# The down product of a feed-forward layer as one level of Strassen's seven block products, and a reordered entry

## The chip, the core and the metric

The kernel runs on one core of a Trainium2 chip. The core has a matrix engine (TensorE, PE in the profile, with its weight loads as PEld), VectorE (DVE), ScalarE (ACT), GpSimd (POOL), and DMA queues that several engines issue; most loads here are issued by SyncE (SP). Each engine works through its own instructions in order, and semaphores tie the engines together. The metric is the device time of one execution in microseconds (us), lower is better: the median of several runs, beside one execution that was profiled.

## What is computed

One layer of a decoder, 512 tokens, model width 2048, all in float32. Everything up to `x + mixed @ w_out` is attention and is left alone by the change; the feed-forward behind it is what matters here (D_FF is 5632):

```python
x = x + mixed @ w_out[l]
h = rmsnorm(x, ln_ffn[l])
gate, up = jnp.split(h @ w_gate_up[l], 2, axis=-1)
x = x + (jax.nn.silu(gate) * up) @ w_down[l]
return rmsnorm(x, ln_final)
```

So "gate and up" is a product of 512 x 2048 by 2048 x 11264, and "down" one of 512 x 5632 by 5632 x 2048.

## The kernel before

**Precision by splitting.** TensorE multiplies in float32r, which keeps fewer bits than float32. Each operand is therefore split into `hi`, its value rounded to float32r, and `lo`, the rest; a product is three matmuls, hi x hi, lo x hi and hi x lo. ScalarE writes `hi` (a Copy), VectorE writes `lo` (a subtraction). A matmul takes a stationary operand of 128 x 128 (`lhsT`), which a weight load brings in, and a moving one of 128 rows and up to 512 columns (`rhs`), and adds into a PSUM bank of 128 x 512.

**Order.** The framework schedules instructions by itself, except those that were pinned to program order: `dma`, and everything issued through `pV`, `pA`, `pG`, `pT` (class `Pinned`, L106 to L118; pinned instructions all carry line L118 in the profile, pinned DMAs L100). The feed-forward is pinned nearly throughout. Exceptions that matter are `rstd_from` (L258) and `row_bc` (L273). Buffers come from pools; a tile of a pool with the option `reuse_waits="tile"` waits for those tiles alone that lay on the same memory before. A pool lays out its tags in the order of their first use.

**Entry of the feed-forward.** The output projection ends in `add_outB` (L933): the residual sum stands in four tiles `x2[c]` of 512 columns (pool `v8`) and is stored to scratch memory `x2s[c]`, the last one on ScalarE's queue (L942). `h2_split` (L887) transposes `x2` on TensorE and scales it to `xh`. `form(p, s)` (L908) makes from `xh` the left sides of the seven products, for half s of the inner dimension, hi and lo side by side in one tile of 512 columns; `form_tile` (L901) says where each lies: for s = 0 those of "1", "7", "2", "5" in `act8` tiles and "4", "6", "3" in three tiles `s8`. `rstd2_make` (L963) computes the norm's row factors on VectorE and ScalarE; `rstd2_bc` spreads them over the partitions with `row_bc`: four diagonal tiles `dg` (VectorE, two buffers), a matmul with `ones` for each, and a copy out (ScalarE). Memory of `v8` is then taken over by pool `ff` (tags `raw2`, `t`, `hct`).

**Gate and up.** This is already one level of a Strassen scheme (Winograd's variant), with products named "1" to "7", in 44 units of 128 gate columns and the 128 up columns that go with them (`Unit`, L984). A unit takes seven slots, one per product in the order `PR` = 1, 7, 2, 5, 4, 6, 3 (NS = 308 slots in all). In each slot `product` issues 8 matmuls of 512 and 8 of 256 columns. The weights of the four blocks ("11", "12", "21", "22") are loaded into `raw` (pool `wp`, 3 buffers) and `raw2`; four right sides are differences that GpSimd makes (`sum`: "7" = 22 − 12, "5" = 12 − 11, "6" = 22 − "5", "4" = 21 − "6"). For each product ScalarE writes the rounded weights twice, to SBUF (`to_hi`, the stationary operand) and to PSUM (`to_hp`, 2 buffers), and VectorE subtracts the latter from the source (`to_lo`). In slot n run hi and lo of n + 1, hp of n + 2 and the product of n. The results are taken out of the banks by the methods `get_...`, added up by `fold` (GpSimd), and go through `gate`, `silu`, `scale_up`, `act`; `store` writes them to scratch memory `aT`. The loop over n at the end of the section has this order written out by hand.

**Down.** `add_down` queues, for 11 groups of 512 inner rows and four chunks c of 512 columns, slabs of 256 rows. The groups come back from `aT` (`load_act`), and are split by `split_act`. `add_tok` (L324) issues for each token block t and each 128 inner rows three matmuls of 512 columns into one bank (L336 to L338); `done` adds the banks into `x2[c]`, which `load_x2` has brought back. `split` (L192) makes hi (L200) and lo (L201) of the weights. The eleventh group comes last, t by t (L1307 to L1309), each t followed by the final norm (`last_col`) and the stores of its rows.

Of the kernel before, what the change touches and what calls it, by code (L numbers as in the profile page):

```python
# [37 lines left out]
def tile_hymba(ctx: ExitStack, tc: tile.TileContext, x, ln_mix, w_in, sb_norm, swa_norm,  # L38
# [234 lines left out]
    def row_bc(col, name, pb=None):  # L273
        pb = pz() if pb is None else pb
        for t in range(NT):
            dg = sm.tile([P, P], F32, tag="dg", name="dg", bufs=2)
            V.tensor_scalar(out=dg, in0=ident, scalar1=col[:, t:t + 1], scalar2=None, op0=ALU.mult)
            mm(pb[:, t * P:(t + 1) * P], lhsT=ones, rhs=dg, start=(t == 0), stop=True,
               skip_group_check=True)
# [880 lines left out]
    def add_down(n):  # L1160
        for c in range(4):
            r0 = n * GF * P

            def done(t, pb, c=c):
                xc = x2[c][:, t, :]
                V.tensor_tensor(out=xc, in0=pb, in1=xc, op=ALU.add)
# [174 lines left out]
```

## Time and profile before

| | us |
|---|---|
| runs, median of 3 | 2109.63 |
| lowest, highest | 2109.22, 2110.27 |
| the profiled execution | 2110.75 |
| its span, first to last instruction | 2109.0 |

| busy in the profiled execution | us | share of the span |
|---|---|---|
| TensorE matmuls | 2072.3 | 98% |
| VectorE | 1489.1 | 71% |
| ScalarE | 1235.1 | 59% |
| GpSimd | 677.7 | 32% |

Counted on TensorE's timeline, the feed-forward begins at 733 us, the down product at 1612 us and its last group at 2056 us. In the rows of the profile, `out<-in` names the tiles written and read, `xN` counts instructions, and a bracket at the end of a timeline row gives the engine's idle time before it and what ended that. `z`, `m` and `o` are the PSUM banks. Rows of matmuls overlap by half, so a matmul's share of time is the distance of two starts, not the row's duration.

### The profile page before, as it was taken

Reading aid. Unit: us, or ns where it says so; the run is one execution under the profiler, and the core shown is the slowest. Engines: PE = TensorE matmul, PEld = TensorE weight load, DVE = VectorE, ACT = ScalarE, POOL = GpSimd, SP = SyncE. Lnnn points to the kernel's source line nnn. Section 1 sums busy time; section 2 is a strip of 40 time slices with the busy share of each in tenths; the row PEclk is TensorE's granted clock in tenths of the full one; section 3 lists DMA queues with packets and bytes.
Section 4 is the critical chain, followed back from the end, with each engine's and each line's share of the span. In section 5 each row is a group of like instructions: output and inputs, shape, how many; then the busy total and the mean of one; then the engine's idle time right before and its main releaser. Section 6 shows DMA issues by size and latency. Waiting matters only on the chain.

```text
span 2109.0 us, 28765 instructions
## 1 busy us (share of the span) xinstructions
PE 2072.3 (98%) x10634; PEld 1760.4 (83%) x10634; DVE 1489.1 (71%) x1953; ACT 1235.1 (59%) x1773; POOL 677.7 (32%) x415
## 2 busy tenths in 40 slices
PE   8999999999999989999999999999999999999998
PEld 7888888888788868888888888888887888888886
DVE  3358888769935778888788788788777545545565
ACT  5347777557723467777777777777775222222232
POOL 0014444200000146666666666666662000000000
PEclk9999999999999989999999999999999999999999
DMA  5332222222242435534544544553454433333332
GB/s 180 91 89 66 66 62 69 73 78 81 85 155 93 156 88 129 135 105 121 135 114 111 135 124 107 130 133 103 125 135 170 165 120 120 120 117 127 127 130 80
DMA packets 285516, 239.94 MB, mean 114 GB/s; under 512 B 10368, under 2 KB 236736, under 8 KB 282816
## 3 DMA queue, kind: packets, MB, share of 16 engines
q1 hardware_dynamic: 284960, 235.97, 37.9%
q8 instruction: 84, 1.38, 0.3%
q0 software_dynamic: 176, 1.06, 0.1%
q10 hardware_dynamic: 240, 1.07, 0.1%
q14 instruction: 56, 0.46, 0.1%
HBM read 218.14 MB, written 19.92 MB: 113 GB/s over the span
## 4 chain that ended last, share of the span: by engine, by line
PE 91%; DVE 4%; DMA 2%; issue 1%; ACT 1%; SPq 0%; POOLq 0%; DVEq 0%; ACTq 0%
PE o L118 22%; PE m L118 17%; PE m L368 4%; PE m L369 4%; PE m L370 4%; PE z L338 4%; PE z L337 4%; PE z L336 4%; PE m L337 4%; PE m L336 4%; PE m L338 4%; PE o L336 3%; PE o L337 3%; PE o L338 3%; DMA raw<-in_w_down_dram 1%
## 5 line engine op out<-in xcount | busy, mean ns | idle before, releaser
L200 ACT ACTIVATE whi<-raw 128x1024 fp32r<-128x1024 f32 x184 | 194.6, 1058 | 435.8 <-PE o L338 204.2
L201 DVE TENSOR_TENSOR wlo<-raw,whi 128x1024 fp32r<-128x1024 f32 x184 | 227.9, 1238 | 287.2 <-ACT whi L200 284.6
L118 POOL TENSOR_TENSOR t<-raw,t 128x1024 f32<-128x1024 f32 x88 | 224.1, 2547 | 270.0 <-ACT hp L118 180.9
L118 DVE TENSOR_TENSOR wlo<-t,hp 128x1024 fp32r<-128x1024 f32 x176 | 214.3, 1218 | 111.9 <-PE o L118 70.4
L118 ACT ACTIVATE whi<-t 128x1024 fp32r<-128x1024 f32 x176 | 186.6, 1060 | 95.1 <-PE o L118 59.8
L118 POOL TENSOR_TENSOR t<-raw,raw 128x1024 f32<-128x1024 f32 x86 | 208.8, 2429 | 52.2 <-DVE wlo L118 43.1
L118 DVE TENSOR_TENSOR wlo<-raw,hp 128x1024 fp32r<-128x1024 f32 x132 | 159.9, 1211 | 43.2 <-issue 38.9
L118 PE MATMUL m<-hca,whi 128*128 128x512 f32 x704 | 185.4, 395 | 4.7 <-ACT whi L118 4.5
L118 PE MATMUL o<-hca,whi 128*128 128x512 f32 x704 | 184.7, 394 | 0.0
L118 ACT ACTIVATE hp<-t 128x1024 fp32r<-128x1024 f32 x176 | 178.1, 1012 | 2.4 <-POOL t L118 2.4
L118 ACT ACTIVATE whi<-raw 128x1024 fp32r<-128x1024 f32 x132 | 139.3, 1055 | 58.4 <-PE m L118 55.0
L368 PE MATMUL m<-hhi,whi 128*128 128x512 f32 x416 | 169.1, 407 | 0.9 <-DVE swv L256 0.9
L369 PE MATMUL m<-hlo,whi 128*128 128x512 f32 x416 | 163.1, 392 | 0.0
L370 PE MATMUL m<-hhi,wlo 128*128 128x512 f32 x416 | 162.8, 391 | 0.0
L118 PEld LDWEIGHTS m<-hca,whi 128*128 128x128 f32 x704 | 127.6, 190 | 28.3 <-ACT whi L118 4.9
L118 PEld LDWEIGHTS o<-hca,whi 128*128 128x128 f32 x704 | 127.5, 190 | 22.8
L118 DVE TENSOR_TENSOR w<-w,rbc 128x512 f32<-128x512 f32 x88 | 139.4, 1585 | 2.3 <-POOL w L118 2.3
L118 ACT ACTIVATE hp<-raw 128x1024 fp32r<-128x1024 f32 x132 | 133.2, 1009 | 3.6 <-DMA raw<-in_w_gate_up_dram 3.0
L337 PE MATMUL z<-wlo,ah 128*128 128x512 f32 x320 | 124.6, 389 | 0.0
L338 PE MATMUL z<-whi,al 128*128 128x512 f32 x320 | 124.5, 389 | 0.0
L336 PE MATMUL z<-whi,ah 128*128 128x512 f32 x320 | 124.2, 389 | 0.0
L118 POOL TENSOR_TENSOR w<-c 128x1024 f32<-128x1024 f32 x44 | 106.8, 2427 | 14.3 <-ACT whi L200 14.3
(318 smaller groups left out, 4952.5 us busy)
## 6 DMA issues: line engine op xcount, KB each, us to landing
raw<-in_w_gate_up_dram SPq DMA_DIRECT2D x352, 256.0 KB, 5.2
raw<-in_w_down_dram SPq DMA_DIRECT2D x36, 1024.0 KB, 5.1
raw<-in_w_in_dram SPq DMA_DIRECT2D x40, 512.0 KB, 3.6
raw<-in_w_in_dram SPq DMA_DIRECT2D x64, 256.0 KB, 3.2
raw<-in_w_out_dram SPq DMA_DIRECT2D x32, 512.0 KB, 3.9
aT<-w SPq DMA_DIRECT2D x44, 256.0 KB, 3.5
araw<-aT SPq DMA_DIRECT2D x11, 1024.0 KB, 7.2
raw<-in_w_down_dram SPq DMA_DIRECT2D x16, 512.0 KB, 6.5
```

Of the source, the lines that this page charges most:

```text
L118: return lambda *a, **k: tc.keep_in_program_order(fn(*a, **k))
L200: ih = A.activation(out=hi, in_=raw, func=AF.Copy)
L201: il = V.tensor_tensor(out=lo, in0=raw, in1=f(hi), op=ALU.subtract)
L336: mm(o, lhsT=lh[:, sl], rhs=hi[:, j, :], start=first, stop=False, skip_group_check=halves)
L337: mm(o, lhsT=lh[:, sl], rhs=lo[:, j, :], start=False, stop=False, skip_group_check=halves)
L338: mm(o, lhsT=ll[:, sl], rhs=hi[:, j, :], start=False, stop=(k == nslab * a - 1), skip_group_check=halves)
L368: mm(o, lhsT=wh, rhs=xh, start=(k == 0), stop=False)
L369: mm(o, lhsT=wh, rhs=xl, start=False, stop=False)
L370: mm(o, lhsT=wl, rhs=xh, start=False, stop=(k == KT - 1))
```

## The change

**Down.** The first ten groups become five pairs of groups, and each pair two passes: pass d takes groups 2(d // 2) and 2(d // 2) + 1 as its two inner blocks, and two chunks of 512 columns, so 1024 columns, as its two column blocks; the tokens are split into halves of 256. Of each inner block of 512 rows the weights come in two chunks i of 256 rows. A pass is 14 slots: seven products in the order `PD` = 1, 7, 6, 4, 5, 2, 3, with two chunks each, and 12 matmuls of 512 columns in a slot. It uses the machinery of the units (`Weights` holds what both share): GpSimd makes four sums of each chunk, ScalarE and VectorE hi, hp and lo. `take` adds the banks into x2, or into `vv` for product "6"; `add_v` adds `vv` to the other three quarters at the end. `Left` makes the left sides: it loads two groups from `aT`, forms the differences in place, and splits them into `act8` tiles `dca`; for the first pair these operations stand on VectorE up to product "4", later mostly on GpSimd. The eleventh group stays as it was and has its weights and its left side loaded and split during pass 9.

**The order.** What to issue in which slot now comes from a table (`at_slot`, `run`), with the stages load, sum, product, take and late, for units and passes alike; slot NS is the first of pass 0. Within the units the slots of the single steps stay as they were, save that the last unit's steps come earlier and that its `fold` is on VectorE. Loads of pass 0 and of its left side start in slot NS − 6.

**The entry.** `form_tile` puts "5", "4", "6", "3" of s = 0 in `act8`, and "1", "7", "2" in `s8`. The first unit's block "21" goes to `raw` in place of `raw2`, and is issued behind sum "5". `rstd2_bc` comes behind product 8 in place of product 7, and its four `dg` are made by ScalarE.

The core of the diff:

```diff
     def row_bc(col, name, pb=None):
-        pb = pz() if pb is None else pb
+        act = pb is not None
+        pb = pb if act else pz()
...
+            if act:
+                A.activation(out=dg, in_=ident, func=AF.Copy, scale=col[:, t:t + 1])
...
     def form_tile(p, s):
         if s == 0:
-            return (act8("hca") if p in "1725" else
+            return (act8("hca") if p in "5463" else
...
-                   if q in ("11", "22") or self.j == 0 and q != "21" else ft("raw2", [P, 8, P], F32, 3))
+                   if q in ("11", "22") or self.j == 0 else ft("raw2", [P, 8, P], F32, 3))
...
-            pG.tensor_tensor(out=self.w4[:, 0:2, :].rearrange("p a (h b) -> p (a h) b", h=2), in0=self.c[:, :, 0:256],
+            (pG if self.j < NFF - 1 else pV).tensor_tensor(out=self.w4[:, 0:2, :].rearrange("p a (h b) -> p (a h) b", h=2), in0=self.c[:, :, 0:256],
...
+    PD = ("1", "7", "6", "4", "5", "2", "3")
+    class Pass(Weights):
...
+        def sum(self, p, i):
+            a, b = {"7": ("22", "12"), "5": ("12", "11"), "6": ("22", "T5"), "4": ("21", "T6")}[p]
...
+            pG.tensor_tensor(out=t, in0=self.raw[a, i], in1=self.t[b[1], i] if b[0] == "T" else self.raw[b, i],
+                             op=ALU.subtract)
...
+        def product(self, pi):
+            p, i = pi
+            if i == 0 and p in "1752":
+                get = (pm, po)[(self.d + (p in "72")) % 2]
+                self.bank[p] = [get(), get()]
+            on = {"6": "1", "4": "7", "3": "5"}.get(p)
+            bk = self.bank[on or p]
+            hi, lo = self.hi.pop(pi), self.lo.pop(pi)
+            x = dc[self.g, p]
+            for part, w in ((0, hi), (256, hi), (0, lo)):
+                for e in range(2):
+                    for t in range(2):
+                        c = part + t * P
+                        pT.matmul(bk[t], lhsT=x[:, 2 * i + e, c:c + P], rhs=w[:, e, :],
...
+        def take(self, p):
...
+            for t in range(2):
...
+                pV.tensor_tensor(out=out, in0=bk[t], in1=out, op=ALU.add)
...
+    class Left:
...
+        def diff(self, eng):
+            self.s3 = ft("t", [P, 4, 256], F32, 3)
+            eng.tensor_tensor(out=self.s3, in0=self.block("11"), in1=self.block("21"), op=ALU.subtract)
...
+        def hi(self, p):
+            dc[self.g, p] = act8("dca")
+            pA.activation(out=dc[self.g, p][:, :, 0:256], in_=self.src(p), func=AF.Copy)
+        def lo(self, p, eng):
+            hl = dc[self.g, p]
+            eng.tensor_tensor(out=hl[:, :, 256:512], in0=self.src(p), in1=f(hl)[:, :, 0:256], op=ALU.subtract)
...
+    for c in range(4):
+        at_slot(NS + (-4, -3, 3, 4)[c], "load", load_x2, c)
+    for d in range(10):
+        b0, u = NS + 14 * d, passes[d]
+        for q, k in (("11", -6), ("12", -5), ("22", -3), ("21", 0)):
+            at_slot(b0 + k, "load", u.load, q, 0)
+            at_slot(b0 + k + (q != "11"), "load", u.load, q, 1)
+        for k, p in ((-3, "5"), (-1, "7"), (1, "6"), (3, "4")):
+            at_slot(b0 + k, "sum", u.sum, p, 0)
+            at_slot(b0 + k + 1, "sum", u.sum, p, 1)
+        for k, p in enumerate(PD):
+            at_slot(b0 + 2 * k + 2, "take", u.take, p)
+    for g in range(5):
+        b0, l = NS + 28 * g, lefts[g]
+        for k in range(2):
+            at_slot(b0 + (-16 if g else -6) + k, "load", l.load, k)
+        if g:
+            order = ((-10, l.hi, "1"), (-9, l.lo, "1", pG), (-8, l.diff, pG), (-7, l.hi, "7"), (-7, l.s1, pG),
+                     (-6, l.lo, "7", pG), (-5, l.s2, pG), (-4, l.hi, "6"), (-3, l.lo, "6", pV), (-2, l.hi, "4"),
+                     (-1, l.lo, "4", pV))
+        else:
+            order = ((-3, l.hi, "1"), (-3, l.lo, "1", pV), (-2, l.diff, pV), (-1, l.hi, "7"), (-1, l.lo, "7", pV),
+                     (0, l.s1, pV), (1, l.s2, pV), (2, l.hi, "6"), (2, l.lo, "6", pV), (3, l.hi, "4"),
+                     (4, l.lo, "4", pV))
+        for k, fn, *args in order + ((4, l.hi, "5"), (5, l.lo, "5", pG), (5, l.hi, "2"), (6, l.lo, "2", pG),
+                                     (7, l.s4, pG), (8, l.hi, "3"), (9, l.lo, "3", pG)):
+            at_slot(b0 + k, "late", fn, *args)
...
+    at_slot(5, "late", rstd2_make)
+    at_slot(8, "late", rstd2_bc)
...
+    units[0].sum("5")
     units[0].load("21")
-    sums(1)
+    units[0].sum("6")
     form("2", 1)
     of(2, "to_hp")
-    for n in range(NS):
+    for n in range(NS + ND):
```

More of the change, by code (lines that the diff above doesn't have):

```diff
@@ L1174, in tile_hymba, with at_slot, run @@
-    down0 = len(queue)
-    for n in range(NG - 1):
-        if n == NG - 2:
-            last_from = len(queue)
-        add_down(n)
-    def load_x2(c):
-        x2[c] = xp.tile([P, NT, 512], F32, tag="x2", name="x2r", bufs=4)
-        dma(out=x2[c], in_=x2s[c])
+    plan = {}
+    def at_slot(n, stage, fn, *args):
+        plan.setdefault((n, stage), []).append((fn, args))
+    def run(n, stage):
+        for fn, args in plan.pop((n, stage), ()):
+            fn(*args)
+    for j in range(NFF):
+        b0, u = 7 * j, units[j]
+        for q in ("22", "12", "11"):
+            at_slot(b0 - 5, "load", u.load, q)
+        at_slot(b0 - 3, "load", u.load, "21")
+        for k, p in enumerate("7564"):
+            at_slot(b0 - 2 + k, "sum", u.sum, p)
+        late = j < NFF - 1
+        for k, fn in ((1, u.get_p1), (2, u.get_p7), (3 if j else 5, u.get_c11), (4, u.get_p75), (6, u.get_u2),
+                      (6, u.get_c22), (7, u.get_c12), (9 if late else 7, u.fold), (10 if late else 8, u.gate),
+                      (11 if late else 8, u.silu), (11 if late else 9, u.scale_up), (12 if late else 9, u.act),
+                      (13 if late else 9, u.store)):
+            at_slot(b0 + k, "take", fn)
@@ new lines, in load_x2 @@
+    def load_x2(c):
+        x2[c] = (side.tile([P, NT, 512], F32, tag="s8", name="x2r", bufs=3) if c < 2 else e8("x2r"))
+        dma(out=x2[c], in_=x2s[c])
+    for c in range(4):
[10 more added lines that the diff above has]
+            at_slot(b0 + 2 * k + 2, "take", u.take, p)
@@ L1184, in tile_hymba @@
+    at_slot(4, "late", form, "3", 1)
+    at_slot(5, "late", rstd2_make)
+    at_slot(8, "late", rstd2_bc)
+    at_slot(NS + 9, "late", lambda: tc.keep_in_program_order(A.preload_act_table_set("natural_log_exp_and_others")))
+    for k in [k for k in plan if k[0] < 0 or k == (0, "sum")]:
+        del plan[k]
+    units[0].sum("5")
     units[0].load("21")
-    for n in range(3, 5):
-        loads(n)
-    sums(1)
+    units[0].sum("6")
     form("2", 1)
     of(2, "to_hp")
-    for n in range(NS):
-        j, k = divmod(n, 7)
-        loads(n + 5)
-        sums(n + 2)
+    for n in range(NS + ND):
+        if n > 1:
+            run(n, "load")
@@ L1194, in tile_hymba @@
         if n:
+            run(n, "sum")
             of(n + 1, "to_hi")
@@ L1200, in tile_hymba @@
         of(n, "product")
[L1201 to L1242 removed]
+        run(n, "take")
+        run(n, "late")
+    run(NS + ND, "take")
+    run(NS + ND, "late")
     open_z("psz2")
[L1246 to L1249 removed]
     gf = const.tile([P, D], F32, tag="swv", name="gf")
```

250 lines of the change are left out of this document (132 added, 118 removed).

## The prediction

> **What bounds the kernel now.** I read the page first, then the busy time by stretches, then TensorE's timeline, and only then the waits at the two places where TensorE stops.
>
> ```profile
> span 2109.0 us, 28765 instructions
> PE 2072.3 (98%) x10634; PEld 1760.4 (83%) x10634; DVE 1489.1 (71%) x1953; ACT 1235.1 (59%) x1773; POOL 677.7 (32%) x415
> PE 91%; DVE 4%; DMA 2%; issue 1%; ACT 1%; SPq 0%; POOLq 0%; DVEq 0%; ACTq 0%
> ...
> 800.00:1600.00 800.00, 800.00 (x4584) 704.02 (x4583) 656.34 (x656) 628.95 (x697) 501.36 (x205) 1.00 0.46 121
> 1660.00:2050.00 390.00, 389.33 (x1717) 321.71 (x1716) 206.73 (x240) 98.21 (x95) 0.00 (x0) 1.00 0.37 124
> 736.00:777.00 41.00, 30.56 (x142) 25.02 (x141) 31.19 (x33) 24.12 (x30) 18.46 (x7) 0.83 0.43 116
> ```
>
> TensorE holds 91% of the chain that ended last. In the stretches (columns: length, then busy time of PE, PEld, DVE, ACT, POOL, granted clock, DMA share, GB/s) it is never idle from 800 to 1600 (gate and up) and hardly from 1660 to 2050 (down). In the first of these VectorE is busy for 82% of the time, ScalarE for 79%, GpSimd for 63%, and still TensorE does not wait; in the second VectorE has 53% and ScalarE 25%. So in the down stage a matmul taken away is time taken away, and three engines have room there. From 736 to 777, the entry of the feed-forward, TensorE idles for 10 us and its clock is 0.83.
>
> The price of a matmul is the distance of starts, since the rows' durations overlap. The first and the last of 101 starts in the down stage, and one slot of gate and up:
>
> ```profile
> 1990.20 0.39 PE L336 MATMUL z<-whi,ah 128*128 128x512 f32 x1
> ...
> 2012.87 0.39 PE L337 MATMUL z<-wlo,ah 128*128 128x512 f32 x1
> ...
> 1100.66 2.79 PE o L118 x16
> ```
>
> (2012.87 − 1990.20)/100 = 0.2267 us for 512 columns. A slot of gate and up has 8 matmuls of 512 and 8 of 256 columns in 2.793 us (308 slots).
>
> **The change, part by part.**
>
> *Matmuls.* Down has 11 groups of 4 x 4 x 4 x 3 = 192 matmuls of 512 columns, 2112 in all. The ten passes replace ten groups: 7 products x 2 chunks x 12 = 168 each, 1680 instead of 1920. The last group keeps its 192. So 240 go: 240 x 0.2267 = **−54.4 us**. The columns of one matmul stay at 512, and one stationary load stands before each, as now. A pass alternates between two banks at each matmul; in the stretch from 1660 to 2050 the bank changes at each third matmul and the distance stays 0.2267, so I take nothing for it.
>
> The Trainium skill, "TensorE: Matmul & The Clock Gate", section "Back-to-back issue gap", gives 131 ns for a sustained stream of 512 columns; by that figure the 240 would be worth an estimated 31.4 us. The trace's 226.7 ns is for these very matmuls and decides.
>
> *Can the other engines feed the passes?* A slot of a pass is 12 x 0.2267 = 2.72 us. Its work, by these rows:
>
> ```profile
> L118 ACT ACTIVATE hp<-t 128x1024 fp32r<-128x1024 f32 x176 | 178.1, 1012 | 2.4 <-POOL t L118 2.4
> L118 ACT ACTIVATE whi<-t 128x1024 fp32r<-128x1024 f32 x176 | 186.6, 1060 | 95.1 <-PE o L118 59.8 <-PE m L118 34.3 <-PE o L338 1.0
> L118 DVE TENSOR_TENSOR wlo<-t,hp 128x1024 fp32r<-128x1024 f32 x176 | 214.3, 1218 | 111.9 <-PE o L118 70.4 <-PE m L118 41.6
> L118 POOL TENSOR_TENSOR t<-raw,t 128x1024 f32<-128x1024 f32 x88 | 224.1, 2547 | 270.0 <-ACT hp L118 180.9 <-DVE wlo L118 78.1 <-DMA raw<-in_w_gate_up_dram 5.9
> L118 POOL TENSOR_TENSOR t<-raw,raw 128x1024 f32<-128x1024 f32 x86 | 208.8, 2429 | 52.2 <-DVE wlo L118 43.1 <-ACT hp L118 6.7 <-DMA raw<-in_w_gate_up_dram 2.4
> L1166 DVE TENSOR_TENSOR x2r<-z,x2r 128x512 f32<-128x512 f32 x80 | 53.0, 685 | 24.1 <-PE z L338 20.3 <-DMA x2r<-x2s 3.8
> L118 DVE TENSOR_TENSOR w<-w,rbc 128x512 f32<-128x512 f32 x88 | 139.4, 1585 | 2.3 <-POOL w L118 2.3
> ...
> 1603.79 0.68 DVE L118 TENSOR_TENSOR w<-w,rbc 128x512 f32<-128x512 f32 x1
> ```
>
> ScalarE: 1.01 + 1.06, and 7 copies for the left side in 28 slots, 7 x 1.06/28 = 0.27: 2.34 us, 86%. VectorE: 1.22, one add (0.69) on average, and two subtractions in 28 slots, some 0.15: 2.06, 76%. GpSimd: 16 sums and 9 left operations in 28 slots, 25 x 2.49/28 = 2.22, 82%. All lie under 2.72. Sums come one slot before their use, one in each of 13 slots in a row at most; the adds into x2 wait for a product that ended as their slot begins, and the bank is wanted two slots later, so the split queued behind them on VectorE is not held. Loads are 5.24 MB a pass, 138 GB/s, near the 121 of gate and up. I take **0** for the 140 slots; bounds 0 and one slot a pass (27 us), if jitter eats GpSimd's lead.
>
> *Entry of the feed-forward.* Today:
>
> ```profile
> 733.25 1.17 PE L118 MATMUL m<-hca,whi 128*128 128x512 f32 x4 [0.24 <-ACT junk L118]
> ...
> 742.19 3.78 PE L118 MATMUL m<-hca,whi 128*128 128x512 f32 x8 [3.12 <-ACT whi L118]
> ...
> 747.48 2.32 PE L118 MATMUL o<-hca,whi 128*128 128x512 f32 x8
> ...
> 760.90 1.19 PE L118 MATMUL m<-hca,whi 128*128 128x512 f32 x4 [1.36 <-ACT whi L118]
> ...
> 764.96 0.68 PE L278 MATMUL m<-dg,ones 128*128 128x128 f32 x4
> 769.24 0.80 PE L278 MATMUL m<-dg,ones 128*128 128x128 f32 x2 [3.59 <-DVE dg L277]
> 771.53 0.80 PE L278 MATMUL m<-dg,ones 128*128 128x128 f32 x2 [1.50 <-DVE dg L277]
> 771.98 2.05 PE L118 MATMUL o<-hca,whi 128*128 128x512 f32 x4
> ...
> 776.47 2.00 PE L118 MATMUL m<-hca,whi 128*128 128x512 f32 x8
> ...
> 731.35 3.89 DMA x2s<-x
> ...
> 735.74 3.36 DMA raw<-in_w_gate_up_dram
> ...
> 726.13 4.75 POOL L118 TENSOR_TENSOR t<-raw 128x1024 f32<-128x1024 f32 x2 [26.52 <-DMA raw<-in_w_gate_up_dram]
> ...
> 759.46 0.20 ACT L262 ACTIVATE rl<-rv 128x4 f32<-128x4 f32 x1 [3.49 <-DVE rv L260]
> ...
> 737.34 1.22 DVE L118 TENSOR_TENSOR xh<-xh 128x1024 f32<-128x1024 f32 x1
> ...
> 772.37 0.60 ACT L281 ACTIVATE rbc<-m 128x512 f32<-128x512 f32 x1 [7.48 <-PE m L278]
> ```
>
> Slot 9 begins at 776.47; nine slots after 733.25 it would be 758.39, so 18.1 us are lost: 3.3 before slot 2, some 2.8 in slots 2 and 3 at half speed (8 matmuls of 512 columns take 3.8 us), 3.2 around slot 7, 7.0 for the row broadcast (764.96 to 771.98), 1.7 in slot 8, again at half speed.
>
> Slot 2 waits for block "21". Its load began when the store of x2[3] ended (731.35 + 3.89 = 735.24), because raw2, the first tile that pool `ff` hands out, lies on the memory of x2[3]. The change puts "21" into `raw`, to be free when sum "5" has read "11". But now sum "5" takes the first tile of `ff`, and I expect the wait to move to GpSimd: sum "5" at 735.3 instead of 728.5, done at 737.8; load 0.5 + 3.4, to 741.5; hp, the form's copy and whi 0.95 to 1.06 each: slot 2 at 744.5, **+2.3**. Queued behind it on GpSimd is only sum "6", which reads "5" anyway; on SP nothing due before slot 2. If the tile lies elsewhere, form "5" is late next (its add ends at 738.6, copy and whi 2.1): 740.7, −1.5. Starting later, TensorE works less of the half-speed stretch (it ends near 748: the eight from 747.48 take 2.3 us, whole ones at full speed 2.0): −1.0. The 3.2 stay: that chain (rstd2 between VectorE and ScalarE) is not touched.
>
> The row broadcast's four `dg` go from VectorE, where they waited behind other work and GpSimd, to ScalarE, behind slot 8. ScalarE shows no 128-column copy here; between its 0.2 us for 4 and 0.6 for 512 columns I take 0.3. Two buffers: two matmul pairs 0.4, two `dg` 0.6, two pairs 0.4, the copy out 0.6 before product 9 gets its bank, with hand-overs some 2.2 instead of 7.0: −4.8, and slot 8 at full clock −1.7. Together **−5.2**, bounds +2 and −13.
>
> *Entry of down.* Today:
>
> ```profile
> 1620.24 11.03 DMA raw<-in_w_down_dram
> ...
> 1627.80 0.39 PE L338 MATMUL o<-whi,al 128*128 128x512 f32 x1
> 1632.48 1.22 PE L336 MATMUL m<-whi,ah 128*128 128x512 f32 x2 [4.30 <-ACT whi L200]
> ...
> 1639.28 0.40 PE L336 MATMUL o<-whi,ah 128*128 128x512 f32 x1
> ...
> 1612.92 3.25 POOL L118 TENSOR_TENSOR w<-c 128x1024 f32<-128x1024 f32 x1 [14.31 <-ACT whi L200]
> ...
> 1625.00:1630.00 5.00, 3.18 (x15) 2.29 (x13) 4.00 (x6) 2.00 (x2) 0.00 (x0) 1.00 1.00 412
> 1630.00:1635.00 5.00, 2.48 (x5) 1.57 (x6) 2.07 (x2) 1.06 (x1) 0.00 (x0) 0.72 1.03 419
> ```
>
> A weight block comes 11 us after its issue, with the 16 DMA engines full at 412 to 419 GB/s; TensorE stops for 4.7 us and then runs at half speed (clock 0.72 in the window behind). From 1627.80 to 1639.28 are 16 starts, 3.6 us by rights: 7.9 us lost. In the new order (NS is the first slot of pass 0) the loads start six slots ahead: 7.3 MB from slot NS−6 to NS−2. At 412 GB/s that is 17.8 us and 2 of latency, against 16.8 to slot NS; the last block, "22", wanted there by sum "7", comes some 2 us late, about what the lead allows.
>
> VectorE is worse off. Because GpSimd makes a sum in each slot from NS−3 to NS+4, the first left side goes to VectorE (7 operations), and so does the last fold. In these 8 slots (22 us) it has 8 splits (9.8), 8 operations from PSUM (5.5), 5 of gate, up and product (3.4 alone) and 8 of 1024 elements (9.8): 28.4. The 13 that read and write SBUF only also wait for GpSimd: w<-w,rbc takes 1.585 on average, and 0.68 when GpSimd is idle (1603.79), so 0.9 more each, 11.7. That is 6 to 18 us too much, less the 3.3 of lead that a split has (it is wanted two thirds into the next slot: 2.72 + 1.81 − 1.22). So 3 to 15 lost; I take 10, and 1 for a chance of half clock: 11 instead of 7.9, **+3.1**. ScalarE's copies of the left side wait for VectorE there, and the next slot's whi stands behind them: the same lag, counted once. The store behind VectorE on SP holds up only x2r loads due 12 slots later.
>
> *The rest.* The last group's weights are split during pass 9 (VectorE and ScalarE under 90%), and GpSimd's load of the last gain now stands behind `al`; VectorE may wait for it some us while TensorE has four free banks, 10.9 us. 0; if that cover were gone, some 3.
>
> Sum: −54.4 − 5.2 + 3.1 = −56.5. The profiled execution took 2110.75 us (span 2109.0), the median of the runs is 2109.63, 1.1 lower. 2110.75 − 56.5 = 2054.25, less 1.1: **2053.1 us**.
>
> **Rivals.** (1) *Both entries run clean*: entry −13, down −5: 2109.6 − 54.4 − 18 = 2037 us. For it: the DMAs start earlier than today. Against: VectorE's 28 us in 22. (2) *The passes lag a slot each* (GpSimd at 82% must keep a strict order, each operation behind the one that waits): +27, or half of that: 2067 to 2080. Against: in gate and up three engines at 82, 79 and 63% cost nothing. (3) *Slower: GpSimd becomes the bound of every pass.* It has 12.5 operations a pass; at 2.49 they take 31 of 38.1 us. From (38.1 + 5.6)/12.5 = 3.5 us each on, ten passes cost the 56 us saved and the change loses; at 3.6 it is 2122. The one of 3.25 (at 1612.92), beside VectorE's splits from SBUF, shows that such durations occur; the means of 2.43 and 2.55 speak against it. (4) *The bank changes slow the stream*: if TensorE paused between banks often enough to be put to half clock for a third of the passes, 381 us would grow by 127: 2180. The row from 800 to 1600 speaks against it: banks change each slot, clock 1.00. The Trainium skill tells of such a case in "TensorE: Matmul & The Clock Gate", section "A second HAM failure mode: psum-queue depth-cycling". (5) *It gives nothing*: the same loss in size as the gain, within 4 us of 2109.6.
>
> **Chances.** Forecast, 2046 to 2062: 0.60. Rival 1, 2035 to 2046: 0.13. Rival 2, 2062 to 2085: 0.19. Rival 3: 0.04. Rival 4: 0.02. Rival 5: 0.02. The range leaves out rivals 3 to 5 (0.08), the cleanest quarter of rival 1 (0.03) and the upper third of rival 2 (0.07): 2038 to 2076. Faster by over 0.2% (about what can be told from no change here): 0.92; within it 0.02; slower 0.06.
>
> **What would show it.** In the profile after: 1872 down matmuls at 0.2267 us; slots of 2.72 us with TensorE busy throughout ten passes; sum "5" of the first unit beginning only after x2s<-x landed; `dg` on ScalarE and a broadcast of some 2 us; VectorE without a gap from NS−3 to NS+6 and TensorE waiting for wlo there. Wrong if TensorE shows a stop in each pass (released by POOL or ACT), or if the distance of starts in a pass is over 0.23.

## The result and the profile after

The changed kernel takes **2062.53 us** (median of 4 runs, 2062.20 to 2062.63) where the kernel before took 2109.95 beside it (4 runs): a ratio of 0.9775, 95% interval 0.9758 to 0.9792. The prediction was 2053.1 with a range of 2038 to 2076: the sign and the range hold, the forecast is 9.4 us too low. The time lies 0.5 us outside the band of 2046 to 2062 that the prediction gave a chance of 0.60, in the band of its rival 2, whose lag in each pass does not show below. The profiled execution took 2062.63 us.

From the page of the changed kernel, then the stretches (length, then busy time of PE, PEld, DVE, ACT, POOL, granted clock, DMA share, GB/s):

```profile
PE 2018.5 (98%) x10394; PEld 1713.1 (83%) x10394; DVE 1484.6 (72%) x1986; ACT 1441.0 (70%) x1992; POOL 1007.0 (49%) x539
```

```profile
1608.00:1640.00 32.00, 23.20 (x83) 16.48 (x83) 31.86 (x25) 18.12 (x20) 22.64 (x9) 0.89 0.52 186
1660.00:1926.00 266.00, 266.00 (x1175) 220.31 (x1174) 194.55 (x204) 214.86 (x221) 216.98 (x88) 1.00 0.41 140
1926.00:1969.00 43.00, 40.30 (x169) 32.38 (x169) 34.83 (x32) 30.32 (x32) 30.39 (x13) 0.96 0.30 94
```

TensorE is 98% busy as before, so the share tells nothing; the stretches do. It is never idle from 1660 to 1926, where VectorE, ScalarE and GpSimd are busy for 73, 81 and 82%. It idles in the first pass, where VectorE has 31.86 of 32 us, and around 1960.

TensorE's timeline of the changed kernel (a bracket is the idle time before the row, and what ended it):

```profile
732.52 1.16 PE L118 MATMUL m<-hcs,whi 128*128 128x512 f32 x4 [0.24 <-ACT junk L118]
...
744.24 2.07 PE L118 MATMUL m<-hcs,whi 128*128 128x512 f32 x4 [5.91 <-ACT whi L118]
...
749.53 2.05 PE L118 MATMUL o<-hca,whi 128*128 128x512 f32 x8
...
767.22 1.16 PE L118 MATMUL o<-hcs,whi 128*128 128x512 f32 x4
...
770.18 0.78 PE L282 MATMUL m<-dg,ones 128*128 128x128 f32 x4
...
772.62 1.20 PE L118 MATMUL m<-hcs,whi 128*128 128x512 f32 x4 [0.69 <-ACT rbc L285]
...
1607.93 0.39 PE L118 MATMUL m<-whi,dca 128*128 128x512 f32 x1
...
1617.54 2.11 PE L118 MATMUL o<-whi,dca 128*128 128x512 f32 x8 [2.44 <-ACT whi L118]
...
1624.30 3.78 PE L118 MATMUL o<-whi,dca 128*128 128x512 f32 x8 [2.06 <-ACT whi L118]
...
1659.49 0.84 PE L118 MATMUL o<-whi,dca 128*128 128x512 f32 x3
...
1926.05 1.98 PE L118 MATMUL m<-whi,dca 128*128 128x512 f32 x8
...
1963.75 1.25 PE L118 MATMUL m<-wlo,dca 128*128 128x512 f32 x4 [2.44 <-DVE wlo L118]
1964.79 3.56 PE L118 MATMUL m<-whi,dca 128*128 128x512 f32 x8
1968.19 1.09 PE L118 MATMUL m<-wlo,dca 128*128 128x512 f32 x4
1969.11 1.98 PE L118 MATMUL o<-whi,dca 128*128 128x512 f32 x8
...
2008.04 0.39 PE L1428 MATMUL z<-lhi,ah 128*128 128x512 f32 x1
```

The rows that start a pass give its length. A pass of 168 matmuls at 0.2267 us takes 38.08 us; what is over is its **loss**. Pass 0 runs from 1607.93 to 1659.49, 51.56 us: loss 13.5. Passes 1 to 7 take 1926.05 − 1659.49 = 266.56 us = 7 x 38.08: no loss. Pass 8 takes 43.06, loss 5.0; pass 9 38.93, loss 0.85. Rows on the other engines of the changed kernel around the stops:

```profile
730.62 0.36 ACTq L946 DMA_DIRECT2D x2s<-x  x1
...
734.76 2.40 POOL L118 TENSOR_TENSOR t<-raw 128x1024 f32<-128x1024 f32 x1 [7.03 <-PE m L118]
...
1613.06 5.71 POOL L118 TENSOR_TENSOR t<-raw,raw 128x1024 f32<-128x1024 f32 x2 [1.57 <-DMA raw<-in_w_down_dram]
1618.73 6.12 POOL L118 TENSOR_TENSOR t<-raw,ty 128x1024 f32<-128x1024 f32 x2
...
1616.46 3.40 DVE L118 TENSOR_TENSOR xd<-xd 128x1024 f32<-128x1024 f32 x1
1619.78 1.21 DVE L118 TENSOR_TENSOR wlo<-t,hp 128x1024 fp32r<-128x1024 f32 x1
...
1622.56 3.38 DVE L118 TENSOR_TENSOR xd<-xd 128x1024 f32<-128x1024 f32 x1
...
1950.42 3.27 DVE L118 TENSOR_TENSOR x2r<-x2r,hct 128x1024 f32<-128x1024 f32 x1
...
1954.74 2.29 DVE L118 TENSOR_TENSOR x2r<-x2r,hct 128x1024 f32<-128x1024 f32 x1
...
1959.40 3.17 DVE L118 TENSOR_TENSOR x2r<-x2r,hct 128x1024 f32<-128x1024 f32 x1
```

The account of the two profiled executions, by their spans (2109.0 and 2060.9, −48.1):

| term | predicted | measured |
|---|---|---|
| 240 matmuls fewer | −54.4 | −54.4 |
| entry of the feed-forward, slot 0 to slot 9 | −5.2 | 40.10 for 43.22: −3.1 |
| entry of down | 11 for 7.9: +3.1 | 13.5 for 7.9: +5.6 |
| stops in the rest of down | 0 | 5.8 for 1.2: +4.6 |
| what lies ahead of slot 0 | 0 | 732.52 for 733.25: −0.7 |
| sum | −56.5 | −48.0 |

The other 1.0 of the 9.4 us is the step from the profiled execution to the median, for which the forecast took off 1.1; here they differ by 0.1.

Three questions follow. What holds slot 2 at 744? What loses 13.5 us in pass 0? And why does pass 8 stop, which the prediction priced at nothing?

### The profile page after: what moved, and what is told of

It reads as the page before. It is cut to its first block, busy times and chain, and to the rows that moved or that the text cites. A ratio compares the mean times of both kernels' runs of the same rounds, so it can differ in the third digit from the quotient of the medians.

```text
span 2060.9 us, 29142 instructions
## 1 busy us (share of the span) xinstructions
PE 2018.5 (98%) x10394; PEld 1713.1 (83%) x10394; DVE 1484.6 (72%) x1986; ACT 1441.0 (70%) x1992; POOL 1007.0 (49%) x539
## 5 line engine op out<-in xcount | busy, mean ns | idle before, releaser
L118 DVE TENSOR_TENSOR wlo<-t,hp 128x1024 fp32r<-128x1024 f32 x236 | 287.9, 1220 | 170.9 <-PE o L118 106.3
L118 ACT ACTIVATE whi<-t 128x1024 fp32r<-128x1024 f32 x236 | 250.2, 1060 | 125.0 <-PE o L118 76.1
L118 POOL TENSOR_TENSOR t<-raw,raw 128x1024 f32<-128x1024 f32 x106 | 277.0, 2615 | 54.7 <-DVE wlo L118 30.8
L201 DVE TENSOR_TENSOR wlo<-raw,whi 128x1024 fp32r<-128x1024 f32 x104 | 130.0, 1250 | 140.0 <-ACT whi L200 137.4
L118 PE MATMUL o<-whi,dca 128*128 128x512 f32 x560 | 140.2, 393 | 4.5 <-ACT whi L118 4.5
L118 PE MATMUL m<-whi,dca 128*128 128x512 f32 x560 | 141.0, 393 | 2.9 <-DVE x2r L118 1.4
L118 PEld LDWEIGHTS o<-hca,wlo 128*128 128x128 f32 x880 | 122.9, 190 | 10.6 <-DVE wlo L118 0.4
L118 PEld LDWEIGHTS o<-whi,dca 128*128 128x128 f32 x560 | 106.0, 190 | 27.4 <-ACT whi L118 5.3
L118 PEld LDWEIGHTS m<-whi,dca 128*128 128x128 f32 x560 | 105.6, 189 | 27.0 <-ACT whi L118 2.3
L118 PE MATMUL o<-hca,wlo 128*128 128x256 f32 x880 | 126.2, 282 | 0.0
```

The lines of the kernel that those rows point to most:

```text
L118: return lambda *a, **k: tc.keep_in_program_order(fn(*a, **k))
L201: il = V.tensor_tensor(out=lo, in0=raw, in1=f(hi), op=ALU.subtract)
```

## The experiments

Each is the changed kernel with the edit shown. "FF entry" is slot 0 to slot 9; the losses, in us, are read from TensorE's timeline as above. The kernel before took 2111.81 beside e1 to e4, 2110.02 beside e5 to e8, 2110.74 beside e9 to e11 and 2108.78 beside e12 (medians), so times of different groups are compared by the ratio, and single steps by the losses. Only the interval of e12 lies clear of that of the change; what the other edits do is read from the trace of one execution each. In the six kernels that leave pass 0 alone (the changed kernel, e1, e3, e4, e5, e9) its loss is 13.5 to 14.5, and in the nine that leave the adds of pass 8 alone that pass loses 3.3 to 5.0: these are the spreads to read differences by.

| kernel | us | ratio to before, 95% | span | FF entry | pass 0 | pass 1 | passes 8, 9 |
|---|---|---|---|---|---|---|---|
| the change | 2062.53 | 0.9775 (0.9758 to 0.9792) | 2060.9 | 40.1 | 13.5 | 0 | 5.0 + 0.9 |
| e1_ff_layout | 2058.21 | 0.9751 (0.9737 to 0.9766) | 2055.1 | 35.3 | 13.6 | 0 | 3.4 + 0.9 |
| e2_early_loads | 2060.18 | 0.9763 (0.9746 to 0.9779) | 2058.2 | 39.9 | 11.9 | 0 | 3.6 + 0.8 |
| e3_addv_later | 2060.20 | 0.9761 (0.9746 to 0.9775) | 2059.0 | 39.3 | 14.2 | 0 | 0 + 2.9 |
| e4_dg_dve | 2067.33 | 0.9794 (0.9780 to 0.9809) | 2065.5 | 42.3 | 14.5 | 0 | 3.5 + 0.9 |
| e5_addv_pool | 2059.51 | 0.9758 (0.9744 to 0.9773) | 2058.8 | 40.1 | 13.9 | 0 | 0 + 3.2 |
| e6_left_pool | 2061.76 | 0.9768 (0.9751 to 0.9784) | 2059.3 | 39.2 | 13.9 | 0 | 3.3 + 0.9 |
| e7_left_pool_early | 2061.13 | 0.9767 (0.9753 to 0.9782) | 2058.8 | 40.0 | 12.8 | 0 | 3.4 + 0.9 |
| e8_fold_pool | 2060.53 | 0.9765 (0.9750 to 0.9779) | 2058.6 | 40.4 | 12.5 | 0 | 3.4 + 0.9 |
| e9_adds_late | 2060.17 | 0.9760 (0.9744 to 0.9777) | 2057.6 | 40.1 | 13.7 | 0 | 0 + 2.1 |
| e10_tail_late | 2061.70 | 0.9768 (0.9753 to 0.9782) | 2061.1 | 39.3 | 8.3 | 5.2 | 4.9 + 0.9 |
| e11_tail_late_early | 2059.54 | 0.9755 (0.9741 to 0.9770) | 2055.8 | 40.1 | 5.1 | 2.7 | 4.9 + 0.9 |
| e12_all | 2052.76 | 0.9736 (0.9722 to 0.9749) | 2051.1 | 35.4 | 9.5 | 2.3 | 0 + 1.0 |

A loss has two parts: stops, and matmuls at half clock behind them. In the record of the granted clock the stretches at 0.5 in pass 0 are 3.41, 6.83 or 10.24 us long, and starts of matmuls are then 0.43 us apart in place of 0.2267. Counting starts over 0.6 us apart as stops and those 0.3 to 0.6 us apart as slow, each less 0.2267 (the rest is under 0.4):

| pass 0 | loss | stops | slow starts |
|---|---|---|---|
| the change | 13.5 | 10.0 | 3.3 |
| e2 | 11.9 | 7.6 | 4.1 |
| e6 | 13.9 | 9.3 | 4.4 |
| e7 | 12.8 | 10.4 | 2.3 |
| e8 | 12.5 | 9.7 | 2.6 |
| e10 | 8.3 | 5.4 | 2.6 |
| e11 | 5.1 | 4.4 | 0.6 |
| e12 | 9.5 | 5.8 | 3.4 |

The 0.6 of e11, whose granted clock is 1.00 throughout pass 0, shows how much of the last column can be small delays at full clock. The stretches at half clock fall differently from one execution to the next, even where nothing was edited. This is why the FF entry takes 39.2 to 39.3 us in e3, e6 and e10 and 39.9 to 40.4 in the change, e2, e5, e7, e8, e9 and e11: slot 2 takes 4.2 to 4.5 us in those three and 5.3 in the others.

### e1_ff_layout: where the first tile of pool `ff` lies

```diff
-                act8("hca") if p in "2546" else ft("hct", [P, 4, 512], F32R))
+                act8("hca") if p in "2546" else first_ff[0])
...
+    first_ff = [ft("hct", [P, 4, 512], F32R)]
     units[0].sum("5")
```

> Only the order in which pool ff hands out memory changes: its first tile becomes hct (first written later), so the tile that sum "5" of the first unit writes no longer lies on x2[3]. Theory (memory): sum "5" no longer waits for the store of x2[3] (lands about 734.6); it starts about 728, block "21" lands about 734, and slot 2 starts at about 740 instead of 744.2, limited by form "5"; the stop ahead of it falls from 6.2 us to about 2, with less of the half clock behind it; slot 9 comes 4 to 7 us earlier, the whole 4 to 7 us shorter (2056 to 2059). Rival (another wait, such as form "5" or block "21" itself, ends as late): slot 2 stays within 1 us of 744.2 and the time within 1 us of 2062.5.

TensorE and GpSimd at slot 2 of e1:

```profile
725.82 4.74 POOL L118 TENSOR_TENSOR t<-raw 128x1024 f32<-128x1024 f32 x2 [26.62 <-DMA raw<-in_w_gate_up_dram]
...
740.53 1.20 PE L118 MATMUL m<-hcs,whi 128*128 128x512 f32 x4 [1.83 <-ACT whi L118]
...
744.00 2.11 PE L118 MATMUL o<-hca,whi 128*128 128x512 f32 x8
```

Sums "7" and "5" now follow each other (x2 in the first row), where the changed kernel's "5" waited until 734.76, just after the store issued at 730.62 had landed (3.9 us later by the same profile). Slot 2 starts at 740.53 instead of 744.24, takes 3.47 us instead of 5.29, and the entry is 4.8 us shorter. The memory theory holds; the rival (slot 2 within 1 us of 744.2) falls. The bracket of the row at 734.76 names PE, not the store: the trace alone would not have settled it.

### e4_dg_dve: the four `dg` back on VectorE

```diff
-            if act:
+            if False:
                 A.activation(out=dg, in_=ident, func=AF.Copy, scale=col[:, t:t + 1])
```

> The four dg of the row broadcast go back to VectorE, still behind product 8; the rest is as in the changed kernel. It measures what this part is worth by itself. My prediction's step (ScalarE takes the broadcast from 7.0 us to 2.2): the broadcast takes 5 to 7 us again and the total is 4 to 5 us longer, 2066.5 to 2068. Rival (the place behind product 8 does it, whatever the engine): within 1.5 us of 2062.5.

The broadcast in e4, on TensorE:

```profile
770.54 0.38 PE L282 MATMUL m<-dg,ones 128*128 128x128 f32 x2
...
773.71 0.67 PE L282 MATMUL m<-dg,ones 128*128 128x128 f32 x2 [1.81 <-DVE dg L281]
775.06 2.07 PE L118 MATMUL m<-hcs,whi 128*128 128x512 f32 x4 [0.69 <-ACT rbc L285]
...
780.35 1.96 PE L118 MATMUL o<-hca,whi 128*128 128x512 f32 x7
```

The first of the four pairs ran ahead of slot 8, at 767.08, and the last still waits 1.8 us for VectorE: 4.5 us from 770.54 to slot 9, less than the 5 to 7 expected, against 2.4 with ScalarE. Slot 9 then runs at half speed (775.06 to 780.35, 2.5 us over). Together 4.6. That the span is 4.6 longer too is partly chance: pass 0 loses 1.0 more and pass 8 1.5 less. It is ScalarE that earns this part, not the place behind product 8.

### e2_early_loads: pass 0's loads earlier

```diff
-        for q, k in (("11", -6), ("12", -5), ("22", -3), ("21", 0)):
+        for q, k in (("11", -6), ("12", -5 if d else -8), ("22", -3 if d else -7), ("21", 0)):
```

> In pass 0 alone the loads of block 12 are issued three slots earlier (NS-8, NS-7 instead of NS-5, NS-4) and those of 22 four slots earlier (NS-7, NS-6 instead of NS-3, NS-2). Pass 0 takes 51.6 us instead of 38.1. Theory A (late loads: sum 7 waits for block 22 until 1613): 3 to 6 of the 13.5 us lost go, sum 7 no longer waits for a DMA, total 2057 to 2060. Theory B (VectorE has more work there than time, and the wait for the DMA lies beside it): less than 1.5 us go, total 2061 to 2062.5, and the stops are put down to VectorE's wlo and get operations.

The loss falls by 1.6 us, to 11.9: between the two theories, and nearer to B; the stops alone fall by 2.4. GpSimd in e2:

```profile
1601.94 6.20 POOL L118 TENSOR_TENSOR t<-raw,raw 128x1024 f32<-128x1024 f32 x2
1613.44 2.38 POOL L118 TENSOR_TENSOR t<-raw,ty 128x1024 f32<-128x1024 f32 x1 [5.29 <-DVE dca L118]
```

Sum "7" starts 11 us earlier than at 1613.06 and waits for no DMA; the next sum waits 5.3 us for VectorE. Most of the loss is still there.

### e6, e7, e8: work from VectorE to GpSimd

```diff
-            order = ((-3, l.hi, "1"), (-3, l.lo, "1", pV), (-2, l.diff, pV), (-1, l.hi, "7"), (-1, l.lo, "7", pV),
-                     (0, l.s1, pV), (1, l.s2, pV), (2, l.hi, "6"), (2, l.lo, "6", pV), (3, l.hi, "4"),
+            order = ((-4, l.diff, pG), (-4, l.s1, pG), (-3, l.hi, "1"), (-3, l.lo, "1", pV), (-1, l.hi, "7"),
+                     (-1, l.lo, "7", pV), (1, l.s2, pV), (2, l.hi, "6"), (2, l.lo, "6", pV), (3, l.hi, "4"),
```

That is e6; e7 has the loads of e2 as well; e8 is e7 with `fold` of the last unit on `pG`, in the slot 8 of the unit in place of 7, gate and silu in 10, scale_up, act and store in 11.

> The first pair's diff and s1 go from VectorE (slots NS-2 and NS) to GpSimd in slot NS-4, where it waited for the loads of block 12 for 8 us; the loads stay as late as they were. VectorE loses 1.2 and 3.4 us of work ahead of and in pass 0. Theory B (VectorE's sum of work sets the loss of 13.5 us): 3 to 6 us of it go. Theory A (the late loads of 22, landed at 1613, set it): under 1.5 us go.

> Both: the early loads of e2 and diff and s1 on GpSimd as in e6. If each hides the other (loads and VectorE both late), the loss of pass 0 falls from 13.5 us to 4 to 7, more than the sum of the two alone. If VectorE alone sets it, the result is that of e6 within 1.5 us.

> As e7, and the fold of the last unit goes back to GpSimd, in slot NS+1, its later steps (gate, silu, scale_up, act, store) two slots later. VectorE loses another 1.8 to 2.2 us of work in pass 0, and its two or three later steps leave the densest stretch; GpSimd's sums of products 6 and 4 come 2.4 us later. Theory B: another 2 to 4 us of the loss go against e7. Rival (GpSimd is then late with its sums): 0 or worse, the stops are put down to GpSimd.

e6 takes 4.6 us of VectorE's work away (diff 1.21, s1 3.40) and gains nothing (13.9): theory B as stated falls. Theory A doesn't take its place: with the loads early too, e7 and e8 gain no more than e2 alone, and their stops are back at 10.4 and 9.7. That is the second case of e7's expectation, and for e8 its rival: the gain against e7 is 0.2, and ScalarE, whose `whi` ends two of TensorE's three longest stops (1.95 and 2.80 us), waits for GpSimd's sums four times in that stretch. Groups of VectorE's work from 1602 to 1634, the changed kernel and then e6 (count, then busy us and mean ns):

```profile
L118 DVE TENSOR_TENSOR dca<-t,dca 128x1024 fp32r<-128x1024 f32 x1 | 2.6, 2590 | 0.0
L118 DVE TENSOR_TENSOR dca<-xd,dca 128x1024 fp32r<-128x1024 f32 x2 | 2.4, 1218 | 0.3 <-ACT dca L118 0.3
...
L118 DVE TENSOR_TENSOR w<-w,rbc 128x512 f32<-128x512 f32 x2 | 2.4, 1203 | 0.0
```

```profile
L118 DVE TENSOR_TENSOR dca<-xd,dca 128x1024 fp32r<-128x1024 f32 x2 | 3.7, 1850 | 0.6 <-ACT dca L118 0.6
L118 DVE TENSOR_TENSOR w<-w,rbc 128x512 f32<-128x512 f32 x2 | 3.4, 1704 | 0.0
...
L118 DVE TENSOR_TENSOR dca<-t,dca 128x1024 fp32r<-128x1024 f32 x1 | 3.4, 3391 | 0.0
```

The same operations take 0.8 + 1.3 + 1.0 = 3.1 us more once GpSimd has more to do beside them. They are those with both inputs in SBUF; `wlo<-t,hp`, with one input in PSUM, stays at 1.21. The rows of the changed kernel above show how: GpSimd's sums end at 1618.77 and 1624.85 (1613.06 + 5.71 and 1618.73 + 6.12), and VectorE's two `xd<-xd`, which started 2.3 us earlier, end at 1619.86 and 1625.94, both 1.09 us later. Each runs when the other has ended; the two engines take turns. In e8 the load has changed sides, as its stretch shows:

```profile
1608.00:1640.00 32.00, 23.30 (x89) 16.82 (x88) 27.79 (x24) 19.96 (x23) 31.84 (x13) 0.95 0.46 150
```

GpSimd is busy for 31.84 of 32 us, VectorE for 27.79, and pass 0 still loses 12.5.

### e10, e11: work out of the stretch

```diff
-                      (6, u.get_c22), (7, u.get_c12), (9 if late else 7, u.fold), (10 if late else 8, u.gate),
-                      (11 if late else 8, u.silu), (11 if late else 9, u.scale_up), (12 if late else 9, u.act),
-                      (13 if late else 9, u.store)):
+                      (6, u.get_c22), (7, u.get_c12), (9 if late else 14, u.fold), (10 if late else 15, u.gate),
+                      (11 if late else 15, u.silu), (11 if late else 16, u.scale_up), (12 if late else 17, u.act),
+                      (13 if late else 17, u.store)):
...
-        at_slot(NS + (-4, -3, 3, 4)[c], "load", load_x2, c)
+        at_slot(NS + (-4, -3, 11, 11)[c], "load", load_x2, c)
```

That is e10; e11 has the loads of e2 as well.

> The last unit's fold, gate, silu, scale_up, act and store come seven or eight slots later (slots NS+7 to NS+10), and the loads of x2[2] and x2[3] behind them (slot NS+11); nothing is given to another engine. Theory C (VectorE's operations between SBUF tiles and GpSimd's sums exclude each other, so that their sum is the bound of pass 0 and moving work from one to the other gives nothing, as in e6 to e8; work must leave the stretch): the four VectorE operations took 6 to 8 us there, so the loss of pass 0 falls from 13.5 to 6 to 9 us. Theory A (the late block 22 sets it): it stays at 12 or more, e11 alone gains. Rival (VectorE is not the bound at all): both stay at 12 or more.

> e10 with the early loads of e2. Theory C: the loss of pass 0 is 4 to 8 us, at most 3 less than e10. If loads and VectorE hid each other, it is 3 us or more less than e10.

Pass 0's loss falls to 8.3 and 5.1, as theory C said. In the changed kernel three of TensorE's stops (before 1621.04, 1624.30 and 1631.21) came behind the tail: VectorE's fold and act, and ScalarE's silu, which waited 2.84 us for VectorE's gate. In e10 these three are gone. The loads of x2[2] and x2[3], which the edit moves too, are not their cause: in the changed kernel they are issued at 1630.88, behind the first two and 0.3 us ahead of the end of the third.

e11 is 3.2 better than e10, a little more than C allowed, but by the stops only 1.0: the one of 2.4 us at ScalarE's `whi`, behind the late "22", is gone, and that of 1.5 at VectorE's `c` is 3.2. The rest is the clock, so that loads and VectorE hid each other is not shown. The stretch from 1608 to 1640 in e10 and in e11:

```profile
1608.00:1640.00 32.00, 27.87 (x113) 21.43 (x112) 30.08 (x27) 22.25 (x23) 28.59 (x10) 0.95 0.40 140
...
1608.00:1640.00 32.00, 28.52 (x127) 22.73 (x125) 32.00 (x32) 25.95 (x29) 21.95 (x9) 1.00 0.30 100
```

In e11 VectorE is still without a gap, but TensorE issues 127 matmuls in place of 83, at full clock. But pass 1 now loses 5.2 and 2.7 us, and e10 gains nothing in all: 8.3 + 5.2 = 13.5. GpSimd in e11:

```profile
1647.55 4.77 POOL L118 TENSOR_TENSOR ty<-raw,rx 128x1024 f32<-128x1024 f32 x2 [5.95 <-DMA aT<-w]
1655.24 4.70 POOL L118 TENSOR_TENSOR t<-raw,raw 128x1024 f32<-128x1024 f32 x2 [2.92 <-DMA raw<-in_w_down_dram]
```

Pass 1's sum "5" wants the memory of a tile of the last unit and waits for its late store; the next sum, "7", waits for loads that stand behind x2[2] and x2[3].

### e3, e5, e9: the adds of pass 8

With `b0` the first slot of pass 9, e3 (e5 has `pG` in its line) and then e9:

```diff
-        at_slot(b0 - 6 + k, "late", passes[8].add_v, k, pV)
+        at_slot(b0 + 5 + k, "late", passes[8].add_v, k, pV)
```

```diff
-        at_slot(b0 - 6 + k, "late", passes[8].add_v, k, pV)
-        at_slot(b0 + 8 + k, "late", passes[9].add_v, k, pG)
+        at_slot(b0 - 6 if k == 0 else NS + ND, "late", passes[8].add_v, k, pV if k == 0 else pG)
+        at_slot(b0 + 8 if k == 0 else NS + ND, "late", passes[9].add_v, k, pG)
```

> The three add_v of pass 8 stay on VectorE but come in slots 5 to 7 of pass 9 instead of slots 8 to 10 of pass 8, at a place where GpSimd has less to do. Theory (VectorE and GpSimd, both on SBUF operands, wait for each other: add_v of 1024 elements took 2.3 to 3.3 us beside GpSimd's 3.4 us): pass 8 takes 38.1 us instead of 43.06 and pass 9 no more than 39.5, total 2057 to 2058.5, add_v about 2.2 us or less each. Rival (it is the plain amount of VectorE's work): the same 4 to 5 us are lost in pass 9 instead, total 2061.5 to 2063.

> The three add_v of pass 8 go to GpSimd, in slots 5 to 7 of pass 9, where GpSimd stood idle for 9.3 us in e3_addv_later; three take some 7.3 us. Theory (what is lost in pass 8 is VectorE's time, and GpSimd has it to spare there): pass 8 takes 38.1 us, pass 9 at most 39.0, the span 4 to 5 us under the 2060.9 of the changed kernel. Rival (the lost time comes back wherever the adds are put): pass 9 takes 41 us or more, the gain is under 2.

> Of the six add_v of passes 8 and 9, the four that touch tokens 256 to 511 move to GpSimd behind pass 9, into the last group, whose first half needs tokens 0 to 255 alone; one stays on VectorE in pass 8, one on GpSimd in pass 9. Theory (e3 and e5: VectorE, or GpSimd beside VectorE's splits of the last group, has no room for the adds anywhere in pass 9 either; they must leave both passes): pass 8 takes 38.1 to 38.6 us, pass 9 at most 39.0, the last group stays at 43.3, the span is 2056.5 to 2058. Rival: the adds delay the last group's second half or the splits, the gain is under 2 us against 2060.9.

In all three pass 8 loses nothing: the adds were its whole stop. VectorE in e3, where GpSimd is idle beside the first add, itself slowed beside the second (3.33 us for an add of its own from 1986.67), and in the way of the third:

```profile
1980.83 1.22 DVE L118 TENSOR_TENSOR x2r<-x2r,hct 128x1024 f32<-128x1024 f32 x1
...
1986.51 1.22 DVE L118 TENSOR_TENSOR x2r<-x2r,hct 128x1024 f32<-128x1024 f32 x1
...
1988.78 2.31 DVE L118 TENSOR_TENSOR x2r<-x2r,hct 128x1024 f32<-128x1024 f32 x1
```

The three took 3.27, 2.29 and 3.17 us in pass 8 of the changed kernel, 8.73 together; at 1.22 they are 3.66. The difference is 5.1 us; the pass lost 5.0 here and 3.3 to 5.0 in the nine kernels with these adds in place, so the size fits and the match to a tenth is chance. But pass 9 has to split the last group's weights on VectorE and pays 2.1 (e3) and 2.3 (e5) more than its 0.9; on GpSimd the adds lengthen those splits, which read SBUF twice as well (2.16 us on average in e5, 1.59 in e3). e9 leaves one add in pass 8, 3.27 us long and at no cost, and pays 1.3 in pass 9. So e3's rival is half right and e5's mostly; e9's span is as expected, its pass 9 is not.

### e12_all: the pieces together

The edits of e1 and e2; in the last unit fold in its slot 12, gate and silu in 13, scale_up, act and store in 14; and

```diff
-        at_slot(NS + (-4, -3, 3, 4)[c], "load", load_x2, c)
+        at_slot(NS + (-4, -3, 8, 9)[c], "load", load_x2, c)
...
-        at_slot(b0 - 6 + k, "late", passes[8].add_v, k, pV)
-        at_slot(b0 + 8 + k, "late", passes[9].add_v, k, pG)
+        at_slot(NS + ND, "late", passes[9].add_v, k, pG)
+        at_slot(b0 - 6 if k == 0 else NS + ND, "late", passes[8].add_v, k, pV if k == 0 else pG)
```

> The pieces that worked, together: hct first in pool ff (e1), the early loads of pass 0 (e2), the last unit's tail late, but two slots earlier than in e11 (slots NS+5 to NS+7) with the loads of x2[2] and x2[3] in NS+8 and NS+9, so that pass 1's sum 5 no longer waits for the store of the tail, and the adds behind pass 9 as in e9, all three of pass 9 among them. Expected from the single runs: entry of the feed-forward 4.8 us less, pass 0 with 5 to 7 us of loss instead of 13.5 and pass 1 with 0 to 1 (e11: 2.7), passes 8 and 9 together with 1 to 2.2 instead of 5.8: 13 to 17 us less, a time of 2046 to 2050. If the pieces hide one another it is 2053 or more; if the tail crowds VectorE again, pass 0 loses 8 or more.

It takes 2052.76 us, faster than both kernels: its ratio to the kernel before, 0.9736 (0.9722 to 0.9749), lies clear of the change's. It misses 2046 to 2050. The entry gives what it gave alone (35.4), and passes 8 and 9 lose 1.0, where e9 lost 2.1. Pass 0 loses 9.5, in the range named for a tail that crowds VectorE again, but of the 4.4 us over e11 only 1.4 are stops; 2.8 are slow starts (two stretches of 3.41 us at half clock, none in e11). Pass 1, expected to lose 0 to 1, loses 2.3. On TensorE, ScalarE and GpSimd of e12:

```profile
1607.82 3.33 PE L118 MATMUL m<-whi,dca 128*128 128x512 f32 x7 [3.19 <-DVE c L118]
...
1632.09 0.63 ACT L118 ACTIVATE w<-w 128x512 f32<-128x512 f32 x1 [3.13 <-DVE w L118]
...
1650.18 4.77 POOL L118 TENSOR_TENSOR ty<-raw,rx 128x1024 f32<-128x1024 f32 x2 [10.25 <-DMA raw<-in_w_down_dram]
```

The second bank of the first product waits 3.2 us for VectorE, which reads it late (`c`), as in e2 and e11 (3.2 each); in the changed kernel it was 1.3. The new stop is the tail's: ScalarE's silu waits 3.1 us for VectorE's gate, the `whi` behind it is late, and TensorE stands for 2.1 us before 1633.71. Pass 1's sum waits for loads that SP issued behind the tail's store.

## Why the prediction was right, and where its sizes were off

**Matmuls: right.** 240 x 0.2267 = 54.4 us went, and passes 1 to 7 keep the distance of 0.2267 to the hundredth. Rivals 2, 3 and 4 all needed a loss in every pass (jitter, GpSimd at 3.5 us an operation, pauses between banks) and fall: seven passes in 266.56 us, clock 1.00. So it was not rival 2 that put the time into rival 2's band. Rival 5, no gain, falls with the result. GpSimd's 217 us in 266 is the 82% that the prediction gave it.

**Entry of the feed-forward: the mechanisms right, −3.1 for −5.2.** Sum "5" did wait for the store of x2[3] (e1), with slot 2 at 744.24 where 744.5 was forecast. The broadcast took 2.4 us for 2.2 and slot 8 nearly full clock (770.18 − 767.22 = 2.96); e4 shows their price. The step that failed is "TensorE works less of the half-speed stretch: −1.0": slots 2 and 3 took 8.1 us (744.24 to 752.37) for 8.4 before, so −0.3 came. The prediction took the end of that stretch, near 748, as fixed. In the changed kernel the granted clock is 0.5 from 742.77 to 749.60; in e3, e6 and e10, with the same stop, until 747.6 to 748.6, and there the two slots take 7.0 to 7.3 us and the −1.0 came. Whether this term holds is chance. The other 1.4 us are small: slot 2 comes 0.5 later after slot 0 than forecast, slots 5 to 7 take 0.5 more, slot 8 and the broadcast 0.2 each.

**Entry of down: right in kind, 13.5 for 11.** VectorE was named as the bound and the late "22" as 2 us; the trace has both. The term mis-sized is the clock: of the 11, 10 were for VectorE and 1 for a chance of half clock; measured are 10.0 us of stops and 3.3 of slow starts. That the 10 was hit is luck, for it was picked from 3 to 15. Taking four operations of VectorE's out of the stretch takes 5.2 us off pass 0 (e10), 4.6 of them stops; the early loads take another 1.0 of stops (e11). The prediction counted GpSimd's time as a delay for VectorE; that the delay goes both ways, so that GpSimd is no way out, it doesn't say: e6 to e8 show that work pushed across comes back as longer operations.

**"The rest: 0": this step failed, by 4.6 us in this execution.** The prediction looked at the last gain and the splits of pass 9, and did not price `add_v` of pass 8: three more operations of 1024 elements on VectorE, both inputs in SBUF, beside GpSimd's sums for pass 9. By the prediction's own rule for such operations they cost 3 x (1.22 + 0.9) = 6.4 us there; 8.7 was measured, and e3, e5 and e9 show that nothing else stopped pass 8. Some 1.6 of the 4.6 us are half clock behind the stop, which six of the nine executions with these adds in place do not have.

So of the 8.5 us by which the terms together missed, some 4.6 are half clock behind stops (0.7, 2.3 and 1.6): the clock was priced too low at each of the three places.

**Rival 1** (both entries clean) is closer in e12 than in the change: there the entry of the feed-forward goes down to 35.4 us, but pass 0 with pass 1 still lose 11.8. What is left of the first stop of pass 0, VectorE's late reading of the last unit's banks, was not taken apart.

## What to carry to other kernels

Where two engines share a way to memory, count the operations that need it as one sum, by stretch, and not by engine: moving two of VectorE's to GpSimd left the stops of pass 0 at 9.3 to 10.4 us, moving four out of the stretch took them from 10.0 to 5.4. That is a gain only if nothing else waits for what moved: in e10 as much came back in pass 1. Price a stop together with the half clock that may follow it, as a range, since the same stop had it in some executions and not in others. Price the odd steps at the ends of a loop (the first fill, the last adds) as carefully as its steady state: all that this prediction missed lay in 135 of 2060 us (the entry, pass 0 and pass 8). And when an order is moved, look at who gets the memory of the tile that now lives longer: here the late tail came back as a wait for its store, or for loads behind it, one pass on.
